# A decoder block on one core: u and the gates in seven products ahead of attention, and the FFN operand formed early

## The chip, the cores and the metric

The kernel runs on one core of a Trainium2 chip. TensorE (PE in the profile) multiplies, VectorE (DVE) and ScalarE (ACT) read its banks and prepare operands, and transfers are issued from three queues: SP, POOL (GpSimd's) and ACT. The metric is the device time of one execution in microseconds. The kernel before takes 2847.26 us, the median of three runs (2846.85 to 2847.84).

## The reference

One layer on 512 tokens of width 2048, all in float32. A wide product of the normed input gives the latents of attention, a gating unit's u and v, and two gates:

```
z = rms_norm(x) @ w_in                    # q_lat 512, kv_lat 512, k_pe 64, u|v 2x1024, gates 2x2048
a = mla(q_lat, kv_lat, k_pe) @ w_o_attn   # 16 heads, causal, rotary part of 64
s = (gelu(u) * (tril(w_s) @ rms_norm(gelu(v)) + b)) @ w_o_sgu
h = x + (sigmoid(g0) * a + sigmoid(g1) * s) @ w_out
f = (silu(n @ w_gate) * (n @ w_up)) @ w_down      # n = rms_norm(h), width 5632
out = rms_norm(h + f)
```

## The kernel before

Products are exact to float32 by splitting: each operand is a high part (a cast on ACT) and a low part (a subtraction on DVE), and `mm3` issues three matmuls for every pair of 128-row blocks (L149 to L151). Weights come in chunks of 128 x 1024 (512 KB): `chunk` loads one on SP (L142) into a raw buffer, casts it on ACT (L143), subtracts on DVE (L144), and gives the raw buffer back. One chunk feeds 24 matmuls of 512 columns.

Stages, in order: the latents and the statistics of x (w_lat), the rotary key (w_kpe), v (w_v, two passes of eight chunks), u (w_u, 16 chunks), the spatial step of the gating unit, attention over eight pairs of heads, the two branch outputs (w_osgu, w_oattn), the gates (w_g1, w_g0: 64 chunks, with x loaded and split a second time, and the branch outputs read back from memory), w_out, the operand of the FFN, the FFN's two wide products, and w_down in five groups of 16 chunks, each group on eight blocks of the hidden layer, and a last part on four blocks.

The FFN's products use seven products in place of eight (`Unit`, `product`, `run`): 2 x 2 blocks of weights and of the operand are combined on DVE first, and a unit of 256 output columns takes seven products of 24 matmuls with 256 columns (L717 to L719). Its operand needs 14 pieces for each of eight blocks (`forms_x`): four subtractions on DVE, a cast on ACT, a subtraction on DVE.

Two arenas hold the tiles. `af` has 52 units of 256 float32 columns: raw chunks take four units, a tile `T()` two, a unit's weights 16. `ar` has 144 units for split operands. `Arena.get` looks at the free aligned places in order and takes the one with the lowest cost, `put` marks a place as the latest freed:

```
cost = (n < self.large and i < self.keep, max(span), -i)
```

So small tiles keep out of the first units where they can, and else the place that was freed longest ago is taken. A scheduler puts the instructions of each engine in order, except those that `pin` fixes. Which place a tile has is fixed when the program is built, and a transfer into a place waits for the last reader of what was there.

In the last stage, the 16 tiles of h take 32 of the 52 units of `af`, and the loads of hidden blocks (`hidden`, on POOL) and of chunks share the rest. In the kernel before, the 88 loads of w_down go round over units 0, 16, 20, 24 and 28. At one place four successive loads go to unit 20.

Of the kernel before, what the change touches and what calls it, by code (L numbers as in the profile page):

```python
# [9 lines left out]
F32 = mybir.dt.float32  # L10
# [14 lines left out]
G = 8  # L25
# [16 lines left out]
NR, NF = 144, 52  # L42
# [3 lines left out]
class Arena:  # L46
# [8 lines left out]
    def get(self, n):  # L55
# [22 lines left out]
def tile_block(ctx: ExitStack, tc, a):  # L78
# [6 lines left out]
    ar = Arena(cst.tile([P, NR * 256], F32R, name="ar"), NR, 112, 14)  # L85
    af = Arena(cst.tile([P, NF * 256], F32, name="af"), NF, 32, 4)
# [35 lines left out]
    def split(src, gain=None, n=512):  # L122
        hi, lo = ar.get(2), ar.get(2)
# [10 lines left out]
    def move(t):  # L134

        s = split(t)
        drop(t)
        return s

    def chunk(src, n=1024):  # L140
        raw, hi, lo = af.get(4), ar.get(4), ar.get(4)
        nc.sync.dma_start(raw[:, :n], src)  # L142
        nc.scalar.copy(hi[:, :n], raw[:, :n])  # L143
        nc.vector.tensor_tensor(out=lo[:, :n], in0=raw[:, :n], in1=hi[:, :n].bitcast(F32), op=ALU.subtract)  # L144
        drop(raw)
        return hi, lo

# [55 lines left out]

# [12 lines left out]
    def load_x(xs, k):  # L216
# [3 lines left out]
        for j in range(2):  # L220
            v = V_MIX + k * 2 + j
            xs.append(split(raw[:, j * 512:(j + 1) * 512], vec[:, v:v + 1]))
# [5 lines left out]
    def x_stats(tb):  # L228
        for c in range(4):
            t = T()  # L230
            nc.sync.dma_start(t, a["x"][tb * P:(tb + 1) * P, c * 512:(c + 1) * 512])
# [23 lines left out]
    for g in range(2):  # L255
        for kp in range(8):
# [5 lines left out]
            if g == 1 and kp < NB:  # L262
                x_stats(kp)
# [3 lines left out]
    rl = rsqrt(lacc, R, 2 * NB, "rl")  # L267

# [34 lines left out]
    raw = af.get(4)  # L303
    nc.sync.dma_start(raw, a["w_kpe"])
    kps = PS()
    for half in range(2):
        wkt = ar.get(4)
        wk = wkt.rearrange("p (k o m) -> p k o m", k=8, o=2)
        rw = raw[:, half * 512:half * 512 + 512].rearrange("p (k m) -> p k m", k=8)
        nc.scalar.copy(wk[:, :, 0, :], rw)  # L310
        nc.vector.tensor_tensor(out=wk[:, :, 1, :], in0=rw, in1=wk[:, :, 0, :].bitcast(F32), op=ALU.subtract)
        for k in range(8):
            w = wk[:, k].rearrange("p o m -> p (o m)")
            for i, x in enumerate(aT[half * 8 + k]):
                nc.tensor.matmul(kps, w, x, start=half + k + i == 0, stop=half * 8 + k + i == KD)
        drop(wkt)
    drop(raw)
    rxb = row_bcast(rx, cst.tile([P, 512], F32, name="rxb"))
    kp0, kpe = T(), T()
    for own, other in ((slice(0, 64), slice(64, 128)), (slice(64, 128), slice(0, 64))):  # L320
        nc.scalar.copy(kp0[own], kps[other])
        nc.vector.tensor_tensor(out=kp0[own], in0=kps[own], in1=kp0[own], op=ALU.add)
    nc.vector.tensor_tensor(out=kp0, in0=kp0, in1=rxb, op=ALU.mult)
    for g in range(2):
        for tb in range(NB):
            nc.vector.tensor_scalar(out=lat[g][tb], in0=lat[g][tb], scalar1=rl[:, g * NB + tb:g * NB + tb + 1],
                                    scalar2=None, op0=ALU.mult)


    vv = [[None, None] for _ in range(NB)]  # L330
    latT = []

    def latents(g):

        rows = []
        for k in range(4):
            ps = PS()
            for tb in range(NB):
                nc.tensor.transpose(out=ps[:, tb * P:(tb + 1) * P], in_=lat[g][tb][:, k * P:(k + 1) * P],
                                    identity=ident)  # L340
            v = (V_Q, V_KV)[g] + k
            rows.append(split(ps, vec[:, v:v + 1]))
        drop(lat[g])
        latT.append(rows)

    for g in range(2):
        banks = [PS() for _ in range(NB)]
        for kp in range(8):
            gemm_tm(banks, a["w_v"][g, kp], kp, aT, kp == 0, kp == 7)
            if g == 0 and kp == 3:  # L350
                latents(0)
                latents(1)
        for tb, ps in enumerate(banks):
            t = T()
            nc.scalar.activation(t, ps, AF.Gelu_apprx_tanh, scale=rx[:, tb:tb + 1])
            vv[tb][g] = t
    qnT, kvT = latT
    rv = rsqrt(sumsq(vv, NB, "sv"), SGUW, NB, "rv")
    for tb in range(NB):
        for g in range(2):  # L360
            nc.vector.tensor_scalar(out=vv[tb][g], in0=vv[tb][g], scalar1=rv[:, tb:tb + 1], scalar2=None,
                                    op0=ALU.mult)

    rope(kp0, kpe)
    kph = ar.get(2)
    kpl = ar.get(2)
# [4 lines left out]
    utd = drm.tile([G, P, 512], F32, name="utd")  # L371
    sgd = drm.tile([G, P, 512], F32, name="sgd")
    for mp in range(4):
        banks = [PS(), PS()]
        for kq in range(4):
            gemm_fm(banks, a["w_u"][mp, kq], kq, aT, kq == 0, kq == 3)
        for i, ps in enumerate(banks):
            t = T()
            nc.vector.tensor_tensor(out=t, in0=ps, in1=rxb, op=ALU.mult)
            nc.scalar.activation(t, t, AF.Gelu_apprx_tanh)  # L380
            nc.scalar.dma_start(utd[mp * 2 + i], t)
            drop(t)
    drop(aT)

    wsT = []
    bsb = []
    for half in range(2):
# [10 lines left out]
        t = T()  # L398
        nc.vector.tensor_copy(t, ps)
        wsT.append(t)  # L400
        bt = T()
        nc.gpsimd.dma_start(bt, a["b_sgu"][half * 512:half * 512 + 512].partition_broadcast(P))
        bsb.append(bt)


    for g in range(G):
        ps = PS()
        gs = slice((g % 4) * P, (g % 4 + 1) * P)
        for n in range(NB):
# [12 lines left out]
    drop(vv, wsT, bsb)
# [114 lines left out]
    ytd = drm.tile([KD, P, 512], F32, name="ytd")  # L537
    ysd = drm.tile([KD, P, 512], F32, name="ysd")

    def load(src):  # L540
        t = T()
        nc.gpsimd.dma_start(t, src)
        return t

    def sgu_out(mp):
        banks = [PS(), PS()]
        for kq in range(2):
            gemm_fm(banks, a["w_osgu"][mp, kq], kq, sgT, kq == 0, kq == 1)
        for i, ps in enumerate(banks):
            t = T()  # L550
            nc.vector.tensor_copy(t, ps)
            nc.gpsimd.dma_start(ysd[mp * 2 + i], t)
            drop(t)
# [4 lines left out]
    for pr in range(NP):  # L558
# [4 lines left out]
        else:  # L563
            drop(qnT, kvT)
            sgT = [move(load(sgd[g])) for g in range(G)]
            sgu_out(0)
        pts = [transposed(prob[e]) for e in range(2)]
# [3 lines left out]
        for e in range(2):  # L571
# [3 lines left out]
            nc.gpsimd.dma_start(ogd[pr * 2 + e], t)  # L575
            drop(t, pts[e][0])
# [9 lines left out]
    oT = [move(load(ogd[k])) for k in range(KD)]  # L586
    for mp in range(8):
        banks = [PS(), PS()]
        for kq in range(4):
# [3 lines left out]
        for i, ps in enumerate(banks):  # L593
            t = T()
            nc.vector.tensor_copy(t, ps)
            nc.gpsimd.dma_start(ytd[mp * 2 + i], t)
            drop(t)


    aT = []  # L600
    mrg = []

    def gate(w, b, mp, load=False, last=False):
        banks = [PS(), PS()]
# [386 lines left out]
```

## Time and profile before

| what | us |
|---|---|
| median of three runs | 2847.26 |
| the profiled execution, and its span | 2848.14, 2846.3 |
| PE busy in the span | 2726.6 (96%) |
| DVE, ACT busy | 1530.8 (54%), 1021.9 (36%) |
| u (384 matmuls of 512 columns) | 199.4 to 287.2 |
| spatial step of the gating unit | 287.2 to 316.4 |
| gates (1536 matmuls of 512 columns) | 844 to 1196 |
| w_out | 1196 to 1377.6 |
| operand of the FFN | 1377.6 to 1449 |
| FFN (7392 matmuls of 256 columns) | 1449 to 2335.8 |
| w_down, from the FFN's last matmul | 2335.8 to 2834 |

A matmul's busy time overlaps that of the next, so the pace of PE is read from the count of matmuls in a stretch. An engine's idle time counts only where the engine is waited for. `PEclk` is the clock that TensorE was granted, 1.00 being 2.4 GHz and 0.50 being 1.2 GHz.

### The profile page before, as it was taken

How to read it: one execution, taken by the hardware profiler on the slowest of the kernel's cores; microseconds unless marked ns; L12 is line 12 of the kernel's file. 1: busy time of each engine (PE TensorE's matmuls, PEld its weight loads, DVE VectorE, ACT ScalarE, POOL GpSimd, SP SyncE). 2: the span in 40 equal slices, each digit the busy share in tenths (PEclk: the TensorE clock that was granted, in tenths of full speed). 3: DMA queues.
4: the chain of work that ended last, by engine and by line, in shares of the span. 5: the costliest groups of instructions: out<-in, count | busy, mean ns of one | idle time of the engine just before them, and what ended most of it. 6: DMA issues, size and time to landing. Idle time of an engine off the chain costs nothing.

```text
span 2846.3 us, 38194 instructions
## 1 busy us (share of the span) xinstructions
PE 2726.6 (96%) x15872; PEld 2420.4 (85%) x15872; DVE 1530.8 (54%) x1937; ACT 1021.9 (36%) x1440; POOL 151.4 (5%) x283
## 2 busy tenths in 40 slices
PE   8999799999999999999579999999999988999998
PEld 6888688887888888888479999999999987888887
DVE  5422566754234334423467777777777764543425
ACT  6231355643123222222344434444444442322213
POOL 0000100011000000001000000000000020000000
PEclk9999899999999999999789999999999999999999
DMA  8222322355335333444123333323232344443322
GB/s 307 85 74 78 131 77 67 123 189 191 119 108 174 114 107 112 127 140 141 45 94 116 117 128 110 126 105 134 104 126 104 134 170 156 148 126 112 126 66 89
DMA packets 101101, 348.75 MB, mean 123 GB/s; under 512 B 13312, under 2 KB 13312, under 8 KB 100928
## 3 DMA queue, kind: packets, MB, share of 16 engines
q1 hardware_dynamic: 76176, 268.99, 28.0%
q0 software_dynamic: 22160, 72.63, 7.7%
q10 hardware_dynamic: 2592, 4.70, 0.5%
q8 instruction: 124, 2.03, 0.3%
q14 instruction: 49, 0.40, 0.0%
HBM read 309.57 MB, written 36.70 MB: 122 GB/s over the span
## 4 chain that ended last, share of the span: by engine, by line
PE 80%; DVE 3%; DMA 2%; issue 2%; ACT 2%; POOL 0%; ACTq 0%; POOLq 0%; DVEq 0%; SPq 0%
PE b L149 16%; PE b L151 16%; PE b L150 16%; PE b L719 10%; PE b L718 10%; PE b L717 10%; DVE af L295 1%; PE b L523 1%; DVE ar L144 1%; DMA ysd<-af 1%; ACT ar L671 0%; DVE ar L672 0%; DMA af<-in_w_g 0%; DMA af<-in_w_down 0%; PE b L502 0%
## 5 line engine op out<-in xcount | busy, mean ns | idle before, releaser
L149 PE MATMUL b<-ar 128*128 128x512 f32 (+1 forms) x2656 | 1019.5, 384 | 50.9 <-ACT ar L143 28.7
L151 PE MATMUL b<-ar 128*128 128x512 f32 (+1 forms) x2656 | 1015.3, 383 | 0.7 <-DVE ar L130 0.6
L150 PE MATMUL b<-ar 128*128 128x512 f32 (+1 forms) x2656 | 1015.4, 382 | 0.0
L717 PE MATMUL b<-ar 128*128 128x256 f32 x2464 | 699.0, 284 | 4.1 <-ACT ar L671 4.0
L719 PE MATMUL b<-ar 128*128 128x256 f32 x2464 | 698.8, 284 | 2.8 <-DVE ar L672 2.8
L144 DVE TENSOR_TENSOR ar<-af,ar 128x1024 fp32r<-128x1024 f32 (+1 forms) x304 | 365.6, 1210 | 621.3 <-ACT ar L143 554.4
L718 PE MATMUL b<-ar 128*128 128x256 f32 x2464 | 698.6, 284 | 0.0
L149 PEld LDWEIGHTS b<-ar 128*128 128x128 f32 x2656 | 501.6, 189 | 153.8 <-ACT ar L143 29.3
L143 ACT CAST ar<-af 128x1024 fp32r<-128x1024 f32 (+1 forms) x304 | 313.8, 1040 | 839.2 <-PE b L150 313.1
L151 PEld LDWEIGHTS b<-ar 128*128 128x128 f32 x2656 | 501.2, 189 | 100.2 <-DVE ar L127 1.5
L150 PEld LDWEIGHTS b<-ar 128*128 128x128 f32 x2656 | 501.7, 189 | 94.1
L717 PEld LDWEIGHTS b<-ar 128*128 128x128 f32 x2464 | 474.5, 193 | 4.5 <-ACT ar L671 4.5
L719 PEld LDWEIGHTS b<-ar 128*128 128x128 f32 x2464 | 474.4, 193 | 3.3 <-DVE ar L672 3.3
L718 PEld LDWEIGHTS b<-ar 128*128 128x128 f32 x2464 | 474.5, 193 | 0.0
L709 DVE TENSOR_TENSOR ar<-af,ar 128x1024 fp32r<-128x1024 f32 x308 | 376.6, 1224 | 160.5 <-ACT ar L708 158.6
L708 ACT CAST ar<-af 128x1024 fp32r<-128x1024 f32 x308 | 318.5, 1047 | 367.8 <-DVE af L729 267.3
L729 DVE TENSOR_TENSOR af<-af 128x1024 f32<-128x1024 f32 x132 | 161.3, 1222 | 3.0
L726 DVE TENSOR_TENSOR af<-b,af 128x256 f32<-128x256 f32 x220 | 92.9, 422 | 37.8 <-PE b L719 33.9
L126 ACT CAST ar<-af 128x512 fp32r<-128x512 f32 x100 | 59.1, 618 | 145.2 <-PE b L151 65.9
L863 DVE TENSOR_TENSOR af<-b,af 128x512 f32<-128x512 f32 x80 | 54.7, 689 | 85.6 <-PE b L151 85.4
L127 DVE TENSOR_TENSOR ar<-af,ar 128x512 fp32r<-128x512 f32 x100 | 66.2, 688 | 61.9 <-ACT ar L126 60.1
L127 DVE TENSOR_TENSOR ar<-b,ar 128x512 fp32r<-128x512 f32 (+1 forms) x96 | 59.9, 663 | 31.2 <-ACT ar L126 31.0
(204 smaller groups left out, 1105.7 us busy)
## 6 DMA issues: line engine op xcount, KB each, us to landing
af<-in_w_gate SPq DMA_DIRECT2D x88, 512.0 KB, 5.2
af<-in_w_up SPq DMA_DIRECT2D x88, 512.0 KB, 5.4
af<-in_w_down SPq DMA_DIRECT2D x88, 512.0 KB, 3.9
af<-in_w_g SPq DMA_DIRECT2D x64, 512.0 KB, 3.5
af<-in_w_oattn SPq DMA_DIRECT2D x32, 512.0 KB, 3.5
af<-in_w_out SPq DMA_DIRECT2D x32, 512.0 KB, 3.5
hidd<-af POOLq DMA_DIRECT2D x44, 256.0 KB, 2.6
af<-hidd POOLq DMA_DIRECT2D x44, 256.0 KB, 3.1
```

The source lines that it names most:

```text
L127: nc.vector.tensor_tensor(out=l, in0=src[:, :n], in1=h.bitcast(F32), op=ALU.subtract)
L143: nc.scalar.copy(hi[:, :n], raw[:, :n])
L144: nc.vector.tensor_tensor(out=lo[:, :n], in0=raw[:, :n], in1=hi[:, :n].bitcast(F32), op=ALU.subtract)
L149: nc.tensor.matmul(ps, sl, mh, start=first, stop=False)
L150: nc.tensor.matmul(ps, sh, mh, start=False, stop=False)
L151: nc.tensor.matmul(ps, sh, ml, start=False, stop=last)
L708: pin(nc.scalar.copy(hv, src))
L709: pin(nc.vector.tensor_tensor(out=lv, in0=src, in1=hv.bitcast(F32), op=ALU.subtract))
L717: pin(nc.tensor.matmul(ps, lo[:, ks], xh, start=first and kp == 0, stop=False, skip_group_check=True))
L718: pin(nc.tensor.matmul(ps, hi[:, ks], xh, start=False, stop=False, skip_group_check=True))
L719: pin(nc.tensor.matmul(ps, hi[:, ks], xl, start=False, stop=kp == 7, skip_group_check=True))
L729: pin(nc.vector.tensor_tensor(out=out, in0=in0, in1=in1, op=ALU.subtract))
```

## The change

1. u and the gates are computed in seven products, ahead of attention: 20 units of 168 matmuls with 256 columns take the place of 1920 matmuls with 512. The operand's pieces are built beside w_v (`x_forms`, six of eight; the last two in `x_rest`). The gates, the latents, v and the rotary key are stored to memory and read back. The spatial step moves into the first two pairs of attention.
2. The branch outputs are multiplied by their gates as they leave the banks, and merged at the attention output. The second load of x and the copy of the attention output in memory go.
3. The FFN's operand is scaled by the norm of the first quarter of the columns (`r0`), and its transposes and six of its eight blocks are formed during w_out. What is missing of the scale (`rest`) is multiplied in before silu (44 more tiles on DVE, through `rxb`) and at the end of w_down (`more`).
4. The first eight hidden blocks are loaded during the FFN's last unit, into operand pieces as these come free (`cut`).
5. `Arena.get` has a new term of cost: places of fewer than eight units in a block of eight that is wholly free cost more than places in a block that is partly held. The limits `keep` and `large` of `af` change, and `keep` is set by stage; in w_down it is 0.

```diff
     def get(self, n, low=False):
         best = None
-        for i in range(0, len(self.free_at) - n + 1, n):
+        end = (self.keep if n >= self.large else 0) or len(self.free_at)
+        for i in range(0, end - n + 1, n):
             span = self.free_at[i:i + n]
             if None not in span:
-                cost = (n < self.large and i < self.keep, max(span), -i)
+                block = self.free_at[i // 8 * 8:i // 8 * 8 + 8]
+                cost = (i,) if low else (n < self.large and i < self.keep, n < 8 and None not in block, max(span), -i)
...
-    af = Arena(cst.tile([P, NF * 256], F32, name="af"), NF, 32, 4)
+    af = Arena(cst.tile([P, NF * 256], F32, name="af"), NF, 0, 16)
...
+    def x_forms(kp):
+        raw, f = af.get(4), af.get(8)
+        nc.gpsimd.dma_start(raw, a["xT"][kp])
+        for j in range(2):
+            v = V_MIX + kp * 2 + j
...
+            nc.vector.scalar_tensor_tensor(
+                out=dst, in0=raw[:, j * 512:(j + 1) * 512].rearrange("p (i m) -> p i m", i=2),
+                scalar=vec[:, v:v + 1], in1=rxb.rearrange("p (i m) -> p i m", i=2), op0=ALU.mult, op1=ALU.mult)
+        drop(raw)
+        forms_x(f, fx)
...
+    def x_jobs():
+        for mp in range(4):
+            yield a["w_u"][mp], u_out(mp)
+        for mp in range(8):
+            yield a["w_g1"][mp], gate_out(g1d, V_B1, mp)
+            yield a["w_g0"][mp], gate_out(g0d, V_B0, mp)
+
+    def x_rest():
+        x_forms(6)
+        x_forms(7)
+    run(x_jobs(), fx, x_rest, {2: lambda: latents_in(0), 4: lambda: latents_in(1)})
...
-        for i, ps in enumerate(banks):
-            t = T()
-            nc.vector.tensor_copy(t, ps)
-            nc.gpsimd.dma_start(ytd[mp * 2 + i], t)
-            drop(t)
+        for ps, t, y in zip(banks, gs, ys):
+            tt(t, ps, t, ALU.mult)
+            tt(t, t, y, ALU.add)
+            drop(y)
+            mrg.append(move(t, low=True))
...
+    order = {(1, 3): 0, (1, 5): 1, (2, 3): 2, (3, 1): 3, (3, 3): 4, (3, 5): 5}
     for c in range(4):
...
+            if c and kp == 2:
+                scaled(c - 1)
+            if (c, kp) in order:
+                f_forms(order[c, kp])
...
+    def f_rest():
+        scaled(3)
+        f_forms(6)
+        f_forms(7)
...
+        row_bcast(rest, rxb)
     def silu(out):
         for t in out:
+            pin(nc.vector.tensor_tensor(out=t, in0=t, in1=rxb, op=ALU.mult))
             pin(nc.scalar.activation(t, t, AF.Silu))
...
+    run(ffn_jobs(), ff, f_rest, {2: lambda: hid.extend(hidden(0, 4)), 4: lambda: hid.extend(hidden(4, 4))})
+    af.keep = 0
     for tb in range(NB):
         for c in range(4):
             h[tb][c] = load(hd[tb, :, c * 512:(c + 1) * 512])
...
             for tb, ps in enumerate(banks):
-                nc.vector.tensor_tensor(out=h[tb][c], in0=ps, in1=h[tb][c], op=ALU.add)
+                more(tb, c, ps)
```

The order of DVE in the second group of w_down and at the start of the third, before. L144 is the subtraction of a chunk, L127 that of a hidden block, L863 adds a finished bank to h; four banks end together with every fourth chunk.

```order
L144 TENSOR_TENSOR ar<-af,ar 128x1024 x8
L863 TENSOR_TENSOR af<-b,af 128x512 x4
L144 TENSOR_TENSOR ar<-af,ar 128x1024 x3
L127 TENSOR_TENSOR ar<-af,ar 128x512 x2
L863 TENSOR_TENSOR af<-b,af 128x512 x4
L127 TENSOR_TENSOR ar<-af,ar 128x512 x6
L144 TENSOR_TENSOR ar<-af,ar 128x1024
L863 TENSOR_TENSOR af<-b,af 128x512 x4
L144 TENSOR_TENSOR ar<-af,ar 128x1024 x6
L863 TENSOR_TENSOR af<-b,af 128x512 x3
```

The same engine at the end of the first group and in the second now. L153 is the subtraction of a chunk, L136 that of a hidden block, L900 adds a bank.

```order
L153 TENSOR_TENSOR ar<-af,ar 128x1024 x4
L900 SCALAR_TENSOR_TENSOR af<-b,rest,af 128x512 x4
L153 TENSOR_TENSOR ar<-af,ar 128x1024 x4
L900 SCALAR_TENSOR_TENSOR af<-b,rest,af 128x512 x3
L136 TENSOR_TENSOR ar<-af,ar 128x512 x2
L900 SCALAR_TENSOR_TENSOR af<-b,rest,af 128x512
L136 TENSOR_TENSOR ar<-af,ar 128x512 x6
L153 TENSOR_TENSOR ar<-af,ar 128x1024 x4
L900 SCALAR_TENSOR_TENSOR af<-b,rest,af 128x512 x3
L153 TENSOR_TENSOR ar<-af,ar 128x1024
```

Before, subtractions of later chunks stand up to eight in a row and ahead of the banks' additions, and those of chunks and hidden blocks are mixed. Now exactly four chunks stand between two sets of additions, the next chunk stands behind them, and all eight hidden blocks stand ahead of a group's first chunk.

The order of DVE where u began before: the last chunks of w_v, the norm of v, the first chunks of w_u, and the first outputs of u (L379).

```order
L144 TENSOR_TENSOR ar<-af,ar 128x1024
L182 RECIPROCAL rvr<-rvr 128x4
L184 TENSOR_TENSOR rvt<-rvr 128x4
L185 TENSOR_TENSOR rvt<-rvt,rvv 128x4
L186 TENSOR_SCALAR rvt<-rvt 128x4
L188 TENSOR_TENSOR rvo<-rvr,rvt 128x4
L361 TENSOR_SCALAR af<-af,rvo 128x512 x8
L144 TENSOR_TENSOR ar<-af,ar 128x1024 x2
L379 TENSOR_TENSOR af<-b,rxb 128x512 x2
```

The same place now. L343 scales half a block of x, the five L117 behind it are the subtractions of `forms_x`, and L375, L394 and L397 prepare the first unit's weights.

```order
L343 SCALAR_TENSOR_TENSOR af<-af,vec,rxb 128x2x256
L343 SCALAR_TENSOR_TENSOR af<-af,vec,rxb 128x512
L375 TENSOR_TENSOR ar<-af,ar 128x1024 x2
L117 TENSOR_TENSOR af<-af 128x256 x3
L203 TENSOR_TENSOR rvt<-rvt,rvv 128x4
L117 TENSOR_TENSOR af<-af 128x256
L204 TENSOR_SCALAR rvt<-rvt 128x4
L206 TENSOR_TENSOR rvo<-rvr,rvt 128x4
L117 TENSOR_TENSOR ar<-af,ar 128x7x256
L343 SCALAR_TENSOR_TENSOR af<-af,vec,rxb 128x2x256
L343 SCALAR_TENSOR_TENSOR af<-af,vec,rxb 128x512
L117 TENSOR_TENSOR af<-af 128x256 x4
```

The last two blocks of x are now loaded, scaled and formed one after the other between the last chunk of w_v and the first outputs of u, where only chunks stood before.

## Rows read from the trace of the kernel before

**Rows 1.** Busy time by stage, one stretch per row; (x) counts instructions.

```profile
core 0: us, PE busy (x) PEld busy (x) DVE busy (x) ACT busy (x) POOL busy (x), PEclk, DMA share, GB/s
199.40:287.20 87.80, 87.80 (x389) 72.64 (x388) 23.70 (x34) 22.78 (x33) 3.80 (x7) 1.00 0.23 76
287.20:293.40 6.20, 0.34 (x2) 0.00 (x0) 0.69 (x1) 0.63 (x1) 1.40 (x2) 0.80 0.38 124
...
303.70:316.40 12.70, 0.23 (x3) 0.07 (x2) 7.25 (x12) 1.66 (x2) 3.75 (x7) 0.67 0.94 312
...
844.00:1196.00 352.00, 351.02 (x1547) 289.90 (x1546) 144.22 (x165) 102.19 (x118) 19.43 (x36) 1.00 0.41 129
...
1377.60:1449.00 71.40, 18.76 (x90) 15.94 (x88) 40.71 (x63) 36.85 (x50) 4.30 (x8) 0.61 0.19 62
1449.00:2335.80 886.80, 886.80 (x7368) 886.80 (x7369) 685.77 (x745) 370.70 (x443) 35.40 (x66) 1.00 0.33 119
2335.80:2356.00 20.20, 0.30 (x4) 0.10 (x2) 11.61 (x17) 9.83 (x14) 5.37 (x10) 0.58 0.93 329
2356.00:2834.00 478.00, 477.96 (x2101) 395.19 (x2102) 196.83 (x253) 120.40 (x158) 17.13 (x32) 1.00 0.36 116
```

**Rows 2.** What PE waited for, 286 to 318 us: total, times, longest.

```profile
PE b L149 <- DVE ar L144: 12.5, 1, 12.5
PE b L396 <- POOL af L392: 5.9, 1, 5.9
```

**Rows 3.** The same, 1376 to 1450 us.

```profile
PE b L691 <- DVE af L684: 45.8, 4, 13.0
```

**Rows 4.** Groups of instructions, 1376 to 1450 us: busy, mean ns.

```profile
L672 DVE TENSOR_TENSOR ar<-af,ar 128x1792 fp32r<-128x1792 f32 x8 | 16.2, 2025 | 14.4 <-ACT ar L671 14.4
...
L671 ACT CAST ar<-af 128x1792 fp32r<-128x1792 f32 x8 | 13.5, 1684 | 9.7 <-DVE af L667 9.7
...
L664 DVE TENSOR_TENSOR af<-af 128x256 f32<-128x256 f32 x8 | 3.4, 425 | 10.7 <-ACT af L698 10.7
```

**Rows 5.** Successive DVE instructions, 2391 to 2399 us: start, length, idle before.

```profile
2391.64 1.23 DVE L144 TENSOR_TENSOR ar<-af,ar 128x1024 fp32r<-128x1024 f32 x1 [4.21 <-ACT ar L143]
2397.53 1.23 DVE L144 TENSOR_TENSOR ar<-af,ar 128x1024 fp32r<-128x1024 f32 x1 [4.66 <-ACT ar L143]
```

**Rows 6.** SP's successive loads, 2392 to 2400 us, both into unit 20.

```profile
2392.89 0.33 SPq L142 DMA_DIRECT2D af<-in_w_down  x1
...
2398.78 0.33 SPq L142 DMA_DIRECT2D af<-in_w_down  x1
```

**Rows 7.** Loads of w_down, 2480 to 2500 us: median us to landing.

```profile
af<-in_w_down SPq DMA_DIRECT2D x4, 512.0 KB, 3.4
```

**Rows 8.** Loads of hidden blocks, 2356 to 2834 us.

```profile
af<-hidd POOLq DMA_DIRECT2D x28, 256.0 KB, 3.0
```

**Rows 9.** Groups of instructions, 2356 to 2834 us.

```profile
L143 ACT CAST ar<-af 128x1024 fp32r<-128x1024 f32 x76 | 79.2, 1053 | 233.2 <-PE b L150 182.9 <-DMA af<-in_w_down 50.2
L863 DVE TENSOR_TENSOR af<-b,af 128x512 f32<-128x512 f32 x80 | 54.7, 689 | 85.6 <-PE b L151 85.4
L127 DVE TENSOR_TENSOR ar<-af,ar 128x512 fp32r<-128x512 f32 x44 | 28.8, 687 | 44.6 <-ACT ar L126 44.6
L126 ACT CAST ar<-af 128x512 fp32r<-128x512 f32 x44 | 25.7, 620 | 102.1 <-PE b L151 65.9 <-PE b L150 26.0 <-DMA af<-in_w_down 9.1
```

**Rows 10.** What PE waited for, 2356 to 2834 us.

```profile
PE b L149 <- ACT ar L143: 19.9, 1, 19.9
```

**Rows 11.** PE's matmuls at the end of two short stalls, idle in brackets.

```profile
30.39 0.50 PE L149 MATMUL b<-ar 128*128 128x512 f32 x1 [1.37 <-DVE ar L130]
...
685.94 0.50 PE L149 MATMUL b<-ar 128*128 128x512 f32 x1 [1.90 <-ACT ar L126]
```

**Rows 12.** Granted clock behind these two stalls, columns as in rows 1.

```profile
30.40:37.20 6.80, 6.80 (x30) 5.59 (x31) 4.35 (x6) 6.71 (x14) 0.00 (x0) 1.00 0.88 281
686.90:693.70 6.80, 6.50 (x15) 4.39 (x15) 3.85 (x4) 2.61 (x3) 0.00 (x0) 0.50 0.57 204
```

More of the change, by code (lines that the diff above doesn't have):

```diff
@@ L68, in get, with cut @@
         return ap
+    def cut(self, ap, n):
+        _, i, m = self.held.pop(id(ap))
+        return [self.piece(j, n) for j in range(i, i + m, n)]
     def put(self, *aps):
@@ L146, in chunk, with load, store @@
         return hi, lo
+    def load(src):
+        t = T()
+        nc.gpsimd.dma_start(t, src)
+        return t
+    def store(dst, t):
+        nc.gpsimd.dma_start(dst, t)
+        drop(t)
     def mm3(ps, sh, sl, mh, ml, first, last):
@@ L267, in tile_block @@
     rl = rsqrt(lacc, R, 2 * NB, "rl")
+    raw = af.get(4)
+    nc.sync.dma_start(raw, a["w_kpe"])
+    kps = PS()
+    for half in range(2):
+        wkt = ar.get(4)
+        wk = wkt.rearrange("p (k o m) -> p k o m", k=8, o=2)
+        rw = raw[:, half * 512:half * 512 + 512].rearrange("p (k m) -> p k m", k=8)
+        nc.scalar.copy(wk[:, :, 0, :], rw)
+        nc.vector.tensor_tensor(out=wk[:, :, 1, :], in0=rw, in1=wk[:, :, 0, :].bitcast(F32), op=ALU.subtract)
+        for k in range(8):
+            w = wk[:, k].rearrange("p o m -> p (o m)")
+            for i, x in enumerate(aT[half * 8 + k]):
+                nc.tensor.matmul(kps, w, x, start=half + k + i == 0, stop=half * 8 + k + i == KD)
+        drop(wkt)
@@ new lines, in tile_block @@
+    drop(raw)
+    rxb = row_bcast(rx, cst.tile([P, 512], F32, name="rxb"))
+    kped = drm.tile([P, 512], F32, name="kped")
+    kp0 = T()
+    for own, other in ((slice(0, 64), slice(64, 128)), (slice(64, 128), slice(0, 64))):
+        nc.scalar.copy(kp0[own], kps[other])
+        nc.vector.tensor_tensor(out=kp0[own], in0=kps[own], in1=kp0[own], op=ALU.add)
+    nc.vector.tensor_tensor(out=kp0, in0=kp0, in1=rxb, op=ALU.mult)
+    store(kped, kp0)
+    for g in range(2):
+        for tb in range(NB):
+            nc.vector.tensor_scalar(out=lat[g][tb], in0=lat[g][tb], scalar1=rl[:, g * NB + tb:g * NB + tb + 1],
+                                    scalar2=None, op0=ALU.mult)
@@ new lines, in tile_block, with form_w, product @@
+    pin = tc.keep_in_program_order
+    def form_w(src):
+        hi, lo = ar.get(4), ar.get(4)
+        hv, lv = (t.rearrange("p (k m) -> p k m", m=P) for t in (hi, lo))
+        pin(nc.scalar.copy(hv, src))
+        pin(nc.vector.tensor_tensor(out=lv, in0=src, in1=hv.bitcast(F32), op=ALU.subtract))
+        return hi, lo
+    FORM = (0, 5, 6, 4, 1, 2, 3)
+    def product(ps, w, xs, first):
+        hi, lo = w
+        for kp, x in enumerate(xs):
+            ks = slice(kp * P, (kp + 1) * P)
+            xh, xl = x[:, :256], x[:, 256:]
+            pin(nc.tensor.matmul(ps, lo[:, ks], xh, start=first and kp == 0, stop=False, skip_group_check=True))
+            pin(nc.tensor.matmul(ps, hi[:, ks], xh, start=False, stop=False, skip_group_check=True))
+            pin(nc.tensor.matmul(ps, hi[:, ks], xl, start=False, stop=kp == 7, skip_group_check=True))
+        drop(w)
@@ new lines, in run, with unit @@
+    def run(jobs, fx, rest, ends, lead=3):
+        jobs = list(jobs)
+        last = 7 * len(jobs) - 7
+        units, ready = {}, {}
+        def unit(n):
+            if n < len(jobs):
+                units[n] = Unit(*jobs[n])
+        unit(0)
+        for g in range(last + 7 + lead + 1):
+            g1, g2 = g - lead, g - lead - 1
+            if g2 >= 0:
+                units[g2 // 7].read(g2 % 7)
+            if g < last + 7:
+                ready[g] = units[g // 7].weights(g % 7)
+                if g % 7 == 6:
+                    unit(g // 7 + 2)
+            if g == lead - 1:
+                rest()
+                unit(1)
+            if 0 <= g1 < last + 7:
+                if g1 == last:
+                    fx[:] = [ar.cut(f, 2) for f in fx]
+                units[g1 // 7].multiply(g1 % 7, ready.pop(g1), fx)
+                if g1 >= last:
+                    drop([f[FORM[g1 - last]] for f in fx])
+                    if g1 - last in ends:
+                        ends[g1 - last]()
@@ L300, in rope @@
         return out
[L303 to L327, printed above, removed]
@@ L330, in tile_block @@
[L330 to L362, printed above, removed]
+    kp0, kpe = load(kped), T()
     rope(kp0, kpe)
-    kph = ar.get(2)
-    kpl = ar.get(2)
+    kph, kpl = ar.get(2), ar.get(2)
     nc.scalar.copy(kph, kpe)
@@ L566, in tile_block @@
             sgu_out(0)
+        if pr < 2:
+            spatial(pr)
         pts = [transposed(prob[e]) for e in range(2)]
@@ L842, in ffn_jobs, with hidden @@
             yield a["w_up"][mp], hidden_out(mp)
-    for _ in run(ffn_jobs()):
-        ffn_operand()
-    drop(fx)
+    hid, h = [], [[None] * 4 for _ in range(NB)]
+    def hidden(k0, n):
+        return [move(load(hidd[k])) for k in range(k0, k0 + n)]
+    run(ffn_jobs(), ff, f_rest, {2: lambda: hid.extend(hidden(0, 4)), 4: lambda: hid.extend(hidden(4, 4))})
+    af.keep = 0
     for tb in range(NB):
@@ L851, in tile_block, with more @@
             h[tb][c] = load(hd[tb, :, c * 512:(c + 1) * 512])
-    def hidden(k0, n):
-        return [move(load(hidd[k])) for k in range(k0, k0 + n)]
+    def more(tb, c, ps):
+        nc.vector.scalar_tensor_tensor(out=h[tb][c], in0=ps, scalar=rest[:, tb:tb + 1], in1=h[tb][c], op0=ALU.mult,
+                                       op1=ALU.add)
     def down(k0, hid):
```

483 lines of the change are left out of this document (224 added, 259 removed).

## The prediction

> **What bounds the kernel now.** Read the stretches by stage first [rows 1]. In u, the gates, the FFN and w_down PE is busy all the time, so there the count of matmuls times their pace is the time: 87.8 us over 389 and 352 us over 1547 give 0.226 and 0.228 us for 512 columns, 886.8 over 7368 gives 0.120 us for 256. DVE and ACT are far from full there. PE is idle in three places: 18.4 us around the spatial step [rows 2], most of the 71.4 us ahead of the FFN, where PE waits four times for the scaling of a quarter of h [rows 1, 3], and 19.9 us ahead of w_down [rows 10]. In w_down itself PE waits for nothing else in 478 us: raw places in several units let loads run ahead. So the change has something to win in the first three stages, and w_down is the stage that it can lose.
>
> **The change, part by part.** The sum is made against the profiled execution, 2848.1 us, 0.9 above the median.
>
> *Seven products for u and the gates.* 1920 x 0.227 = 436 us become 3360 x 0.120 = 404: -32. The units' preparation hides as in the FFN (DVE 686 of 887 us there [rows 1]), the gates needing no more of it.
>
> *The start of u.* Every unit's first product needs all eight operand blocks. Six are built beside w_v, with DVE at 32 us in 90 there. The last two need room in `ar` that w_v's operand gives back only at its end, and both loads of x go through one place in `af`, behind stores of v on POOL. So behind the last bank come, one after the other: a store and a load (3.0 and 3.4 as in [rows 8, 7]), two scalings (0.69 each by the nearest row), four subtractions 1.7, cast 1.7, subtraction 2.0 [rows 4, 9], then a load and the same 6.8 again. That is about 25 us; the product over the six ready blocks covers some 2 to 3. I take 22 idle and 2.5 for the half clock behind, +24.5. Bounds: 8, if the last two loads slip ahead, and 32.
>
> *Spatial step.* The 18.4 us go, with some 4 us at half clock around them. What is late next is the first chunk of attention, a load, cast and subtraction of 5.7 us at most: -16 (-8 to -22). In attention the step now lies beside DVE's 187 of 274 us; +4 (0 to 10).
>
> *FFN operand.* In 1377.6 to 1449 PE does 64 transposes and 26 matmuls; some 68 us are lost, and 3 more to the half clock behind. Now the last quarter alone is late: additions 0.7, four squares and four scalings of 0.6 to 0.7 on ACT 5.5, transposes and copies 3, two blocks of subtractions, cast and subtraction (5.4, the second overlapping half: 8.5), the broadcast of `rest` 2 to 4. About 21, with clock 2.5; 48 transposes now inside w_out cost 5. Together -42 (-30 to -50). In w_out's last quarter forms of 5.4 us stand ahead of chunks on DVE while its loads go through one place: +8 (0 to 20). The 44 extra multiplications, 30 us of DVE, lie beside 200 us of idle DVE in the FFN: 0 (0 to +8).
>
> *Smaller.* x's statistics share the start with the loads of weights: +2 (0 to 4). No second x, no copy in memory: -2.
>
> So all that comes before w_down is worth -54.
>
> *w_down.* Follow the new cost by hand. h takes units 0 to 15, 20 to 31 and 48 to 51. Free are 16 to 19, in a block that is partly held, and 32 to 47, two blocks wholly free, which cost more. `chunk` gives its raw place back before the next asks, so every chunk gets unit 16, all 88, and the hidden blocks from the ninth on share it in pairs (16 and 18). A load must then wait until DVE has subtracted the chunk before it. What such a chain takes stands in the trace, where two loads go to unit 20: the subtraction ends at 2392.87, the load is issued at 2392.89, the next subtraction begins 5.89 us behind the last, and the next load at 2398.78 [rows 5, 6]: 3.4 load, 1.05 cast, 1.23 subtraction and the hand-offs [rows 7, 9]. PE eats a chunk in 24 x 0.227 = 5.44 us. So:
> - within four chunks, 3 x 0.45, in 20 sets: +27.
> - at the end of a set, the new order on DVE puts the next subtraction behind the last bank's addition: 0.69 + 1.23 + 0.1 = 2.0 us of idle PE, 15 times: +30.
> - at the end of a group, four pairs of hidden blocks go through the same unit, 3.0 + 0.62 + 0.69 + 0.15 = 4.46 each, then a chunk of 5.89, against 5.44 of PE work: 18.9 idle, three times, and 10 once, with two pairs: +67.
> - the start of w_down, from the FFN's last output: 22 us where 20.2 are [rows 10]: +2.
> - the last part needs 8 chunks at once. Each takes 5.5 (two half casts and subtractions): 44, then 12 of its 16 sums, against 49 of PE work: +30.
> - clock: behind 1.37 us of idle PE the granted clock stayed at 1.00, behind 1.90 it went to 0.50 for 6.8 us [rows 11, 12]: 15 matmuls where the other stretch has 30, so 3.4 lost. The chain hides half. Of the 15 stops of 2.0 us I count half, 13, and for the six long ones 12: +25 (0 to 45).
>
> Together +181. Bounds: with a load of 2.9 a chunk would be as short as PE's work and, the clock kept up, only the ends of sets and groups, the start and the last part remain, near +130; with 4.5 for a load, as where several are in flight, each set of four loses 3 x 1.1 more, near +250. I take 181, by the row that is the same chain.
>
> The Trainium skill, "DMA: Bandwidth & Descriptors" (Anatomy of one DMA), gives a transfer on POOL's queue 2.0 us and bytes over 436 GB/s: an estimate of 3.2 us for a chunk and 2.6 for a hidden block, against 3.4 and 3.0 here. By that a chunk would take 5.7 and w_down lose about 165. The same section says that a wait stands at the issuing sequencer, ahead of the transfer; the two loads through unit 20 agree, the second being issued 0.02 us behind the subtraction's end.
>
> Sum: 2848.1 - 54 + 181 = 2975; by the median 2974. I write 2975.
>
> **Rivals.**
> 1. *The chain is hidden within a group.* Loads land alone in 2.9 to 3.0, and the clock stays up: only the ends, the start and the last part cost, 27 + 13 less: 2935. For it: the loads are never crowded now. Against: 3.4 was measured with only four loads in 20 us.
> 2. *Faster.* The ends of groups are covered too: the casts and subtractions run many chunks ahead of PE in `ar`, as before, where DVE stood 13 chunks ahead of the additions, so that the one unit is idle when the hidden blocks come. Then w_down is what it was, and 2848 - 54 = 2794. It decides where a chunk takes under 4.4 us, since only 16 x 1 us of lead cover an end; it wins from a loss in w_down of 54 us or less. Against it: the 5.89 of [rows 5], and additions that now stand ahead of the next chunk.
> 3. *The clock falls at every stop.* All 15 stops and the waits in the last part cost 3.4 us, and behind each stop the chain meets PE late: +41. With the start of u at its upper bound, +8, about 3024. For it: 1.90 us sufficed [rows 11, 12]; against: that stop was followed by another, PE waiting 0.3 us again.
> 4. *The seven products bring nothing* since the units wait for the stores of gates, or w_out's loads through one place lose 20: 3005.
>
> The Trainium skill, "TensorE: Matmul & The Clock Gate", describes a kernel in which a wait for loads sends every tile back to the slow clock, since its default is the slow one and activity releases it. By that rule the third rival would be the likeliest: 3024. The trace agrees for one stall of 1.90 us and not for one of 1.37, and no run here shows 2.0 us repeated.
>
> **How the numbers follow.** Forecast 0.55; first rival 0.15; faster 0.06; third 0.14; fourth 0.08; 0.02 for no change. A difference of 0.2% (5.7 us) is what a measurement tells from none. The range, 2905 to 3030, takes in the first, third and fourth cases and the bounds of w_down less their outer parts. Slower 0.92, the same 0.02, faster 0.06.
>
> **What would show it.** In w_down of the changed kernel, SP's loads wait for DVE's subtraction some 80 times, each issued within 0.1 us of its end; DVE's subtractions follow each other by 5.8 to 5.9 us; PE waits for L153 or its cast some 70 times, with five waits of 10 to 20 us; the stretch from the FFN's last matmul to the end takes about 690 us against 510. The gates and u take 404 us with a stall of 15 to 25 at their start, and PE's idle time ahead of the FFN is about 21. It would be wrong if several loads of w_down are under way at once, if DVE's subtractions come closer than 5.4 us, or if w_down's stage is under 560 us.

## The result and the profile after

The changed kernel takes 3051.25 us (median of four runs, 3047.51 to 3057.87) against 2847.55 for the kernel before: 1.0717 times as long, 95% interval 1.0697 to 1.0736. Slower was forecast, but 2975 with a range to 3030. The profiled execution has 3052.1 us, its span 3050.3.

Busy time by stage of the changed kernel, in the columns of [rows 1]: the start of u, the other matmuls of u and the gates, the two branch outputs up to the end of w_osgu, the start of the FFN, the FFN, the start of w_down, its first group, the end of that group, and the last part's beginning.

```profile
217.10:241.60 24.50, 6.74 (x26) 5.25 (x24) 17.59 (x28) 10.49 (x13) 2.14 (x4) 0.55 0.20 71
241.60:645.60 404.00, 403.00 (x3336) 402.80 (x3337) 303.65 (x331) 184.74 (x227) 27.87 (x52) 0.99 0.36 130
...
959.70:1106.60 146.90, 107.45 (x375) 81.43 (x376) 47.43 (x57) 30.59 (x38) 28.53 (x53) 0.87 0.47 151
...
1480.20:1497.00 16.80, 2.16 (x10) 1.63 (x9) 15.33 (x26) 9.23 (x11) 0.00 (x0) 0.57 0.17 63
1497.00:2379.60 882.60, 882.60 (x7346) 882.55 (x7346) 699.23 (x782) 361.76 (x437) 29.95 (x56) 1.00 0.33 119
2379.60:2417.50 37.90, 7.74 (x51) 7.33 (x49) 13.13 (x22) 10.77 (x17) 11.77 (x22) 0.65 0.55 172
2417.50:2513.70 96.20, 91.71 (x383) 72.02 (x384) 30.65 (x32) 16.77 (x17) 1.06 (x2) 0.98 0.27 88
2513.70:2533.30 19.60, 0.44 (x3) 0.04 (x1) 5.74 (x10) 4.96 (x8) 3.22 (x6) 0.58 0.33 107
...
2972.40:3002.80 30.40, 15.15 (x32) 9.12 (x32) 9.39 (x15) 8.52 (x18) 0.00 (x0) 0.53 0.30 104
```

What PE waited for in the whole changed kernel, the three largest rows (us, times, longest); they answer to [rows 2, 3, 10].

```profile
PE b L167 <- ACT ar L152: 147.0, 34, 26.1
PE b L167 <- DVE ar L153: 53.9, 24, 7.6
PE b L167 <- ACT ar L135: 26.7, 13, 3.7
```

L152 and L153 are the cast and the subtraction of a chunk, L135 the cast of a split tile. Four numbers place the change. The FFN's last matmul starts at 2391.1 us instead of 2335.8, so 55 us are lost ahead of w_down, where 54 were to be won; from there to the end it takes 659.2 us instead of 510.5, 149 more, where 181 were forecast. Within the first part the products keep their promise (3336 matmuls in 404.0 us, 0.121 each), and the FFN is as it was. The row nobody expected is the third: 375 matmuls of 512 columns, some 85 us of work by [rows 1], take 147 us.

The single place in w_down, read as in [rows 5, 6]: DVE's subtractions of two successive chunks, and SP's load behind each (start, length, idle before).

```profile
2562.57 1.23 DVE L153 TENSOR_TENSOR ar<-af,ar 128x1024 fp32r<-128x1024 f32 x1 [3.90 <-ACT ar L152]
2568.31 1.22 DVE L153 TENSOR_TENSOR ar<-af,ar 128x1024 fp32r<-128x1024 f32 x1 [4.51 <-ACT ar L152]
```

```profile
2563.83 0.33 SPq L151 DMA_DIRECT2D af<-in_w_down  x1
...
2569.56 0.33 SPq L151 DMA_DIRECT2D af<-in_w_down  x1
```

A load is issued 0.03 us behind the end of each subtraction, and the next subtraction comes 5.74 us behind the last. SP's waits from 2300 us on say the same of the groups' loads (L151):

```profile
SPq L151 <- DMA af<-in_w_down: 229.5, 75, 5.1
SPq L151 <- DVE ar L153: 191.6, 75, 4.3
```

75 times it waits for a load and then for a subtraction. In the trace each of the 88 loads of w_down is issued 0.03 us behind a subtraction, and no two of them are under way at once.

In the stretch of w_osgu the chain is another one. ACT's cast, DVE's subtraction and PE's next matmul, for one chunk and the cast and matmul of the next:

```profile
1065.80 1.05 ACT L152 CAST ar<-af 128x1024 fp32r<-128x1024 f32 x1 [1.27 <-PE b L169]
...
1075.61 1.04 ACT L152 CAST ar<-af 128x1024 fp32r<-128x1024 f32 x1 [1.27 <-PE b L169]
```

```profile
1066.88 1.23 DVE L153 TENSOR_TENSOR ar<-af,ar 128x1024 fp32r<-128x1024 f32 x1 [0.22 <-ACT ar L152]
```

```profile
1068.16 0.50 PE L167 MATMUL b<-ar 128*128 128x512 f32 x1 [2.45 <-DVE ar L153]
...
1077.97 0.50 PE L167 MATMUL b<-ar 128*128 128x512 f32 x1 [2.44 <-DVE ar L153]
```

Here the cast does not wait for a load but for PE's last matmul on the chunk before, because it writes to the place that this chunk's high part still holds. PE then stands still for cast and subtraction, 2.44 us, every 9.8 us. Most of these stops bring the clock down; the granted clock between the stops at 1058.3 and 1065.7, and behind the one that ends at 1077.97, columns as in [rows 1]:

```profile
1060.00:1062.00 2.00, 2.00 (x6) 1.52 (x6) 0.00 (x0) 0.00 (x0) 0.00 (x0) 0.50 0.69 234
1062.00:1064.00 2.00, 2.00 (x9) 1.59 (x8) 1.02 (x2) 1.33 (x3) 0.03 (x1) 0.80 0.02 8
1064.00:1065.40 1.40, 1.40 (x8) 1.07 (x6) 0.91 (x3) 0.53 (x1) 0.51 (x1) 1.00 0.23 91
...
1078.00:1083.70 5.70, 5.70 (x24) 4.40 (x24) 1.04 (x2) 0.62 (x1) 1.61 (x3) 1.00 0.41 159
```

Behind 11 of the 13 stops for a subtraction in this stretch it falls to 1.2 GHz for some 3 us, and a chunk costs 9.8 us instead of 5.44. Behind the two that end at 1020.27 and 1077.97 (2.39 and 2.44 us) it stays at 2.4 GHz, and the chunk costs 8.1 to 8.2. Walking the rule of the arena `ar` through the changed program shows where this comes from: the 14 chunks of w_osgu behind attention all put their high part on unit 116, the only free four units above the limit `keep` = 112, while their low parts go round. In the kernel before nothing is free above the limit at that time, so both parts go round. The same walk shows whose place it is: the two parts of the rotary key hold units 116 and 118 while the 16 parts of the gating unit's result are placed, two of these go below the limit for it, and the key is given back just ahead of the 14 chunks. In the kernel before, the key stands at 76 and 78. No run separates this.

### The profile page after: what moved, and what is told of

Its sections match the earlier page's. It is cut to its first block, busy times and chain, and to the rows that moved or that the text cites. A ratio compares the mean times of both kernels' runs of the same rounds, so it can differ in the third digit from the quotient of the medians.

```text
span 3050.3 us, 41608 instructions
## 1 busy us (share of the span) xinstructions
PE 2761.0 (91%) x17320; PEld 2481.5 (81%) x17320; DVE 1742.5 (57%) x2194; ACT 1102.3 (36%) x1541; POOL 197.4 (6%) x369
## 4 chain that ended last, share of the span: by engine, by line
PE 49%; DMA 8%; issue 5%; DVE 3%; ACT 3%; POOL 0%; ACTq 0%; POOLq 0%; SPq 0%; DVEq 0%
PE b L385 9%; PE b L386 9%; PE b L387 9%; PE b L167 8%; PE b L169 7%; PE b L168 7%; DMA af<-in_w_down 5%; DVE ar L153 2%; DMA af<-hidd 2%; ACT ar L152 2%; DMA af<-in_w_out 1%; POOL af L159 0%; ACT ar L135 0%; DVE ar L136 0%; ACT ar L331 0%
## 5 line engine op out<-in xcount | busy, mean ns | idle before, releaser
L385 PE MATMUL b<-ar 128*128 128x256 f32 x3584 | 1018.6, 284 | 20.3 <-ACT ar L331 11.5
L387 PE MATMUL b<-ar 128*128 128x256 f32 x3584 | 1017.6, 284 | 2.5 <-DVE ar L117 2.5
L386 PE MATMUL b<-ar 128*128 128x256 f32 x3584 | 1017.5, 284 | 0.0
L167 PE MATMUL b<-ar 128*128 128x512 f32 (+1 forms) x2016 | 796.2, 395 | 235.6 <-ACT ar L152 147.0
L168 PE MATMUL b<-ar 128*128 128x512 f32 (+1 forms) x2016 | 782.9, 388 | 0.0
L169 PE MATMUL b<-ar 128*128 128x512 f32 (+1 forms) x2016 | 761.9, 389 | 3.8 <-DVE ar L153 2.8
L385 PEld LDWEIGHTS b<-ar 128*128 128x128 f32 x3584 | 691.5, 193 | 21.7 <-ACT ar L331 12.1
L387 PEld LDWEIGHTS b<-ar 128*128 128x128 f32 x3584 | 691.4, 193 | 3.1 <-DVE ar L117 3.1
L386 PEld LDWEIGHTS b<-ar 128*128 128x128 f32 x3584 | 691.6, 193 | 0.0
L375 DVE TENSOR_TENSOR ar<-af,ar 128x1024 fp32r<-128x1024 f32 x448 | 544.4, 1223 | 251.3 <-ACT ar L374 249.8
L167 PEld LDWEIGHTS b<-ar 128*128 128x128 f32 x2016 | 391.1, 194 | 344.9 <-ACT ar L152 168.6
L374 ACT CAST ar<-af 128x1024 fp32r<-128x1024 f32 x448 | 459.5, 1046 | 480.7 <-DVE af L397 371.6
L153 DVE TENSOR_TENSOR ar<-af,ar 128x1024 fp32r<-128x1024 f32 (+1 forms) x224 | 268.5, 1204 | 593.8 <-ACT ar L152 581.7
L152 ACT CAST ar<-af 128x1024 fp32r<-128x1024 f32 (+1 forms) x224 | 230.6, 1034 | 721.9 <-DMA af<-in_w_down 368.0
L169 PEld LDWEIGHTS b<-ar 128*128 128x128 f32 x2016 | 390.0, 193 | 94.2 <-DVE ar L153 17.8
L168 PEld LDWEIGHTS b<-ar 128*128 128x128 f32 x2016 | 391.8, 194 | 70.5
L397 DVE TENSOR_TENSOR af<-af 128x1024 f32<-128x1024 f32 x192 | 234.6, 1222 | 4.2
L394 DVE TENSOR_TENSOR af<-b,af 128x256 f32<-128x256 f32 x320 | 134.5, 420 | 23.5 <-PE b L387 20.6
L136 DVE TENSOR_TENSOR ar<-af,ar 128x512 fp32r<-128x512 f32 x108 | 72.3, 690 | 126.5 <-ACT ar L135 116.9
L135 ACT CAST ar<-af 128x512 fp32r<-128x512 f32 x108 | 65.4, 619 | 208.9 <-DMA af<-hidd 70.0
L400 ACT COPY af<-b 128x256 f32<-128x256 f32 x128 | 47.4, 370 | 170.6 <-PE b L387 138.2
L900 DVE SCALAR_TENSOR_TENSOR af<-b,rest,af 128x512 f32<-128x512 f32 x96 | 72.0, 750 | 61.0 <-PE b L169 61.0
```

The costliest lines, as they stand in the source:

```text
L167: nc.tensor.matmul(ps, sl, mh, start=first, stop=False)
L168: nc.tensor.matmul(ps, sh, mh, start=False, stop=False)
L169: nc.tensor.matmul(ps, sh, ml, start=False, stop=last)
L374: pin(nc.scalar.copy(hv, src))
L375: pin(nc.vector.tensor_tensor(out=lv, in0=src, in1=hv.bitcast(F32), op=ALU.subtract))
L385: pin(nc.tensor.matmul(ps, lo[:, ks], xh, start=first and kp == 0, stop=False, skip_group_check=True))
```

## The experiments

Each was timed against the kernel before on the same chip; times are medians. Theory A is that these single places make the loss. All but e4 and e8 start from the changed kernel. They use a switch `pack` for the new term of `Arena.get`.

**e1: more places in w_down.** By the walk, chunks and hidden blocks now share five places of four units (16, 32, 36, 40 and 44), where the expectation says six.

```diff
+    af.pack = False
     af.keep = 0
     for tb in range(NB):
         for c in range(4):
             h[tb][c] = load(hd[tb, :, c * 512:(c + 1) * 512])
```

> The changed kernel, with the new term of the arena's cost switched off for af from w_down on, so that chunks and hidden blocks rotate over six places instead of one. Theory A (the one place paces w_down): w_down's stretch goes from 659 us back to some 510, the total from 3051 to 2900 (2885 to 2915). Rival (the additions with the factor rest, or slower transfers, cost the time): the total stays above 3000.

2900.22 us, ratio 1.0186 (1.0171 to 1.0201): 151 less than the changed kernel. From the FFN's last matmul to the end it is 507.9 us. PE's wait at the start of w_down, and its only one from 2420 us on, are

```profile
PE b L168 <- ACT ar L153: 11.4, 1, 11.4
...
PE b L170 <- DVE ar L154: 0.2, 1, 0.2
```

The start is 8.5 us shorter than before [rows 10], and what comes behind it takes 496.2 us where 490.3 were (510.5 less 20.2). So the factor `rest` in the additions and the new order, which are still there, can cost some 6 us here, not 150. The loss in w_down is the place.

**e2: the operand arena's places in the branch outputs.** The limit goes to 0 there. The new term must go as well: with it left in, a walk of the rule finds a hole at unit 48 for all 16 chunks.

```diff
+            ar.keep, ar.pack = 0, False
             sgT = [move(load(sgd[g])) for g in range(G)]
...
+    ar.keep, ar.pack = NX, True
     facc = cst.tile([P, 4 * NB], F32, name="facc")
```

> The changed kernel, with the operand arena ar taking the place freed longest ago during the two branch outputs (its limit keep at 0 and the new term off there), so that the high parts of the w_osgu chunks no longer go to one place. Theory A (a chunk's cast waits until PE has done with the chunk before, 2.8 us each): the stretch 960 to 1107 loses its 14 stalls of 2.8 us and the low clock, 50 to 62 us, the total 2990 to 3000. Rival (the loads of gates and stores of the merged branch on POOL hold PE up): less than 15 us, 3036 or more.

2993.83 us, 57 less than the changed kernel, ratio 1.0522 (1.0502 to 1.0542). 355 matmuls now take 86 us, the clock stays up:

```profile
959.70:1046.00 86.30, 81.68 (x355) 65.73 (x354) 32.48 (x43) 19.69 (x27) 24.56 (x46) 1.00 0.60 203
```

**e3: both.**

```diff
+            ar.keep, ar.pack = 0, False
             sgT = [move(load(sgd[g])) for g in range(G)]
...
+    af.pack = False
     af.keep = 0
```

> Both edits together. Theory A: the two losses lie in stages apart and add up: 3051 - 150 - 56 = 2845 (2825 to 2860), about the time before. Rival (a loss moves to a later stage): 2880 or more.

2842.34 us, ratio 0.9983 (0.9973 to 0.9992): 208.9 less than the changed kernel, where 151.0 and 57.4 make 208.4. The two losses add up and nothing moves to a later stage.

**e4: the kernel before with one place in w_down.**

```diff
+    block = [af.get(4) for _ in range(4)]
+
     def hidden(k0, n):
...
+    drop(block)
     gf = []
```

> The kernel before, with four of the five free places of four units held during w_down, so that all chunks and hidden blocks share one. Theory A: w_down takes the 150 us more that it takes in the changed kernel, 2995 (2970 to 3030), with subtractions 5.8 to 5.9 us apart. Rival (in the changed kernel the new additions and the order add to it): less than 100 us, under 2950.

3015.53 us, ratio 1.0589 (1.0571 to 1.0607): 168 more. The stretch behind the FFN takes 680.8 us, more than the changed kernel's 659.2. DVE's subtractions in it, 2560 to 2570 us:

```profile
2562.61 1.23 DVE L144 TENSOR_TENSOR ar<-af,ar 128x1024 fp32r<-128x1024 f32 x1 [4.62 <-ACT ar L143]
2568.38 1.23 DVE L144 TENSOR_TENSOR ar<-af,ar 128x1024 fp32r<-128x1024 f32 x1 [4.54 <-ACT ar L143]
```

The same chain in the other kernel, 5.77 us. What it costs more lies at the start, where the first eight hidden blocks go through the one place too, which the changed kernel loads during the FFN: the longest wait is 48.1 us, where the changed kernel's start has 26, and 22 is the difference of the two stretches.

```profile
PE b L149 <- ACT ar L143: 137.5, 26, 48.1
```

**e5: the old rule of `ar` from attention on.** The line of e2 stands further ahead.

```diff
+    ar.keep, ar.pack = 0, False
     qs, qp = q_proj(0)
```

> Both edits of e3, with ar's old rule (keep 0, no new term) already from attention on, where the chunks of w_uq and w_ukv share two places in e3. Theory A (the two places make the first matmul behind each pair of heads late): the 1.43 us gap in each pair goes back to 1.1 and the gaps in the first two pairs shrink, 4 to 12 us less than e3, 2830 to 2838. Rival (those gaps are the scores' own chain on DVE and ACT): 2842 within 3.

2831.87 us, ratio 0.9947 (0.9934 to 0.9959): 10.5 less than e3. PE's waits for the subtraction of a chunk, from 655 us to the end of attention, first e3, then e5:

```profile
PE b L168 <- DVE ar L154: 10.2, 10, 2.4
```

```profile
PE b L168 <- DVE ar L154: 1.6, 1, 1.6
```

So 8.6 of the 10.5 us are these waits, about one in each pair of heads.

**e6: the limit of `af` one quarter of w_out later.** The rest is as in e5.

```diff
-        if c == 2:
+        if c == 3:
             af.keep = 32
```

> e5, with the limit keep of af set to 32 one quarter of w_out later, so that its chunks have three to six places for longer. Theory A (the loads of w_out through one place, with the forms ahead of their subtractions on DVE, cost 16 us in the last quarter): 8 to 14 us less than e5. Rival (the forms on DVE alone delay the chunks): less than 4 us.

2809.17 us, ratio 0.9864 (0.985 to 0.9877): 22.7 less than e5, more than theory A said. PE's largest waits from 1300 us to the end of w_out, first e5, then e6:

```profile
PE b L168 <- ACT ar L153: 10.7, 3, 9.5
```

```profile
PE b L813 <- ACT af L849: 0.7, 1, 0.7
```

By the times of the same matmuls in both traces, the stall of 9.5 us and the half clock behind it (some 6 us long) are worth 13. Another 5 come at the FFN's last products, where e5 and then e6 have

```profile
PE b L386 <- DVE af L395: 4.1, 1, 4.1
```

```profile
PE b L386 <- DVE af L395: 0.7, 1, 0.7
```

The changed kernel has this stop too, 4.0 us. Why the later limit shortens it was not taken apart, nor where the last 4 to 5 us come from.

**e7: the loads of w_v ahead of the first unit's on SP.** The rest is as in e6. Only the loads' order on SP changes (`pin` is `keep_in_program_order`); in `chunk` this holds during w_v alone.

```diff
-        nc.sync.dma_start(raw[:, :n], src)
+        pin(nc.sync.dma_start(raw[:, :n], src))
...
-                nc.sync.dma_start(self.raw[:, kq * 1024:(kq + 1) * 1024], w[kq])
+                pin(nc.sync.dma_start(self.raw[:, kq * 1024:(kq + 1) * 1024], w[kq]))
```

> e6, with the loads of w_v and of the units kept in the order of the program on SP, so that the first unit's loads no longer stand ahead of nine chunks of w_v. Theory A (PE's stalls of 7.2, 3.2 and 3.2 us in w_v come from loads of the first unit that wait at the head of SP's queue): 10 to 15 us less than e6. Rival (they come from raw places held by stores of the latents): less than 4 us; the first unit's weights come later and may cost a few at the start of u.

2799.21 us, ratio 0.983 (0.9817 to 0.9843): 10.0 less than e6. PE's waits from 120 to 180 us, e6 and then e7:

```profile
PE b L168 <- ACT ar L153: 9.8, 2, 7.1
PE b L170 <- DVE ar L154: 2.5, 1, 2.5
```

```profile
PE b L170 <- ACT ar L155: 6.1, 2, 3.3
```

Half of the wait was the order on SP, and by the times of the same matmuls 7 of the 10 us are won by the start of u. The rest of the wait stays; whether stores of the latents cause it, as the rival has it, was not tested.

**e8: the kernel before with one place for the high parts of w_osgu.** `chunk` is given one place, kept for all of `sgu_out`.

```diff
-        raw, hi, lo = af.get(4), ar.get(4), ar.get(4)
+        raw, hi, lo = af.get(4), one if one is not None else ar.get(4), ar.get(4)
...
+            place = [ar.get(4)]
             sgu_out(0)
```

> The kernel before, with the high parts of all w_osgu chunks written to one place of the operand arena. Theory A: PE waits for cast and subtraction behind each of the 14 chunks after attention, 14 x 2.3 to 2.8 = 32 to 39 and up to 20 for the clock: 2885 to 2907. Rival (such a wait is hidden by work of the next stage): less than 15 us.

2899.36 us, ratio 1.018 (1.0166 to 1.0194): 51 more. PE's waits from 590 to 760 us, where the kernel before has 2.2 us:

```profile
PE b L149 <- DVE ar L144: 29.0, 12, 2.5
PE b L149 <- ACT ar L126: 5.7, 2, 3.5
```

35 us of waits, 2 of which were there before. The other 18 to 19 fit the clock, which falls to 0.50 for some 3 us behind 9 of the 12 stops for a subtraction; they were not measured apart. The single place alone makes this loss in a kernel that has nothing else of the change.

**e9: one more block of x formed beside w_v.** The rest is as in e7.

```diff
                 if kp in (1, 3, 5):
                     x_forms(kp // 2 + 3)
+                if kp == 6:
+                    x_forms(6)
...
     def x_rest():
-        x_forms(6)
         x_forms(7)
```

> e7, with the seventh of the eight operand blocks of x formed behind the seventh chunk of w_v's second pass, so that only one block is left for the start of u. Theory A (PE's wait there is two blocks formed one after the other): PE's idle time between w_v and the second product of u falls from 18 us by the length of one block, 5 to 9 us, and the clock is back sooner, 6 to 11 us less than e7, 2789 to 2793. Rival (the first unit's weights, or the last block's own chain of load, scaling and forming behind the last bank, set the time): 2797 or more.

2792.89 us, ratio 0.9806 (0.9793 to 0.9819): 6.3 less than e7, at the edge of what was expected, and the intervals of the two just meet. It is the fastest of all, 55 us ahead of the kernel before. PE's waits from 200 to 245 us fall from 17.4 us (e7) to 9.3:

```profile
PE b L390 <- ACT ar L335: 11.2, 2, 7.1
PE b L390 <- DVE ar L380: 3.7, 1, 3.7
PE b L392 <- DVE ar L118: 2.5, 2, 1.3
```

```profile
PE b L392 <- DVE ar L382: 4.7, 1, 4.7
PE b L392 <- ACT ar L335: 3.3, 1, 3.3
PE b L394 <- DVE ar L118: 1.3, 1, 1.3
```

## Why the prediction was wrong

The direction and the main mechanism were right, and the size was not: 204 us slower instead of 127. The step that failed is "So all that comes before w_down is worth -54". It came out as +55.

*What was missing there.* The prediction walked the new rule of places through `af`, found the single place of w_down, and did not walk `ar`, nor the places of any stage ahead of w_down but w_out's last quarter. The branch outputs stood in the sum at nothing but the second x and the copy in memory. They cost 57 us (e2) through one place for the high parts, shown again in the kernel before (e8). The two shared places in attention cost 10.5 (e5), against the +4 that stood there for the spatial step. In w_out "+8 (0 to 20)" stands against the 22.7 of e6, of which some 15 lie in w_out, within the bound, and 5 at the FFN's last products. And the first unit's loads at the head of SP's queue cost 10 (e7), most of it in w_v, where the prediction looked at DVE's and `ar`'s room for the operand blocks but not at what the units' loads are queued ahead of. Together 101 us, 8 of them foreseen in w_out, against the 109 by which the step missed. What is left, some 16 us, was not taken apart; longer gaps in the first pairs of attention and the 6.1 us of waits that e7 leaves in w_v are among it.

*What was right there.* The seven products take 404 us, as worked out. The start of u lost 24.5 less 26 x 0.12, 21 us, by the first row after, against +24.5. The FFN starts 16.8 us behind w_out instead of 71.4 [rows 1], against some 21. With the places out of the way (e7) the kernel is 49 us faster than before, and -54 was the sum; so the second rival, 2794, is close to e7's 2799 and e9's 2793, though not by its mechanism: the places had to be given back.

*w_down*, +181 forecast and +149 measured, item by item. The ends of groups: 19.6, 19.2, 20.0 and 10.4, 69 us, against 67. The start: 26.4 against 20.2, +6 against +2. The five groups, 96.2 to 100.4 us against 87.0 of work: +51, where 57 stood for sets and their ends and most of 25 for the clock. The last part is what is left of the 149, 23 against 30. Two of the prediction's sums are smaller by their own terms (18.3 us for an end of four pairs, 64 in all, not 67; 23.4 for the chain at the start of u, not 25), which changes nothing here. The mis-sized terms are two. A load landed in 3.3 us here (median), not 3.4, and the chain took 5.74 instead of 5.89. And the stop of 2.0 us behind each set hardly shows: behind the additions PE finds matmuls that need only the high part, which is cast before, and goes on with those. PE's matmuls at the end of such a set, while DVE subtracts from 2580.37 to 2581.59:

```profile
2580.00 0.39 PE L167 MATMUL b<-ar 128*128 128x512 f32 x1
2580.23 0.39 PE L168 MATMUL b<-ar 128*128 128x512 f32 x1
2580.46 0.39 PE L167 MATMUL b<-ar 128*128 128x512 f32 x1
...
2581.64 0.50 PE L169 MATMUL b<-ar 128*128 128x512 f32 x1
```

L169, the one with the low part, comes when the subtraction has ended, 0.12 us late. So PE stands still for only 4 to 6 us in a group (96.2 less 91.71 in the first, 22 in all), and for a chunk's cast or subtraction 29 times in all of w_down, not some 70. The five longest stops within the groups, 1.66 to 2.08 us, each follow a load that took 5.0 to 5.4 us. The load ahead of the longest, and the granted clock behind it and behind the one of 1.79 us that ends at 2965.16:

```profile
af<-in_w_down SPq DMA_DIRECT2D x1, 512.0 KB, 5.4
```

```profile
2595.90:2599.00 3.10, 3.10 (x9) 2.42 (x8) 0.00 (x0) 0.25 (x1) 0.00 (x0) 0.53 0.48 169
2965.20:2968.60 3.40, 3.40 (x15) 2.83 (x16) 1.92 (x2) 0.00 (x0) 0.00 (x0) 1.00 0.36 105
```

The other three left it at 1.00 too. That is why the third rival, the clock falling at every stop in w_down, did not come about in the groups. Its mechanism did in w_osgu, and in the last part, where PE stops six times for 2.2 to 3.7 us and the row from 2972.4 to 3002.8 us in the section on the result has 0.53.

*The other rivals.* The chain was not hidden within a group; no load of w_down landed in less than 3.0 us. The seven products did bring their gain, and w_out's part of the fourth rival was real, some 15 us.

## What to carry to other kernels

Where tiles share an arena, a rule that prefers one place also decides how many loads can be under way: walk it through every stage and every arena, and look for a place that comes up each time. A raw buffer with one place costs the difference between the chain (load, cast, subtraction) and the work of a chunk, and far more where another kind of tile shares it and PE has to wait for that (69 of the 149 us in w_down); an operand buffer with one place costs cast and subtraction in full, since the multiplying engine itself must finish first. Before summing the gains of a change, price the helper it alters wherever that is called.

## What the runs showed of the hardware

In w_osgu, 11 of 13 stops of 2.39 to 3.34 us brought the granted clock to 0.50 for some 3 us; the two that did not, 2.39 and 2.44 us, are as long as most that did. In w_down one stop of 2.08 us brought it down, four of 1.66 to 1.79 us left it at 1.00; before, 1.90 had brought it down and 1.37 had not [rows 11, 12]. Of the 51 us that the single place cost in e8, 33 are added waits and the rest fits the clock. Order within one product can hide a wait: matmuls that need only the first of two prepared parts gave the second 1.6 us.
